# A scan's decayed inputs formed on VectorE from the transposed tile, with decay times step size, in place of a second product on GpSimd

## The chip, the cores and the metric

The kernel runs on one core of one Trainium2 chip. The metric is device time in microseconds (us) per execution. The engines of the core are TensorE (PE in the profile; PEld is its weight load), VectorE (DVE), ScalarE (ACT), GpSimd (POOL) and SyncE (SP, which here only issues transfers). Each works through its own queue in order and waits for the others by semaphores.

## What is computed

One layer of a hybrid block on 512 frames: a retention branch and a Mamba-2 (SSD) branch, merged by gates, then an output projection. The change lies in the SSD branch. Cut to it:

```python
dt = softplus(dt_raw + dt_bias)                 # (b, s, groups, heads per group): the step size
a = dt * (-exp(a_log))
xdt = xs * dt[..., None]
def step(state, inp):                           # over chunks
    xc, bc, cc, ac = inp                        # xc is a chunk of xdt
    acum = cumsum(ac, axis=1)
    ...
    y = einsum('blsg,blsgh,bsghp->blghp', cb, decay, xc)            # inside the chunk
    y = y + einsum('blgn,bghpn->blghp', cc, state) * exp(acum)[..., None]
    tail = exp(acum[:, -1:] - acum)
    state = (state * exp(acum[:, -1])[..., None, None]
             + einsum('bsgn,bsgh,bsghp->bghpn', bc, tail, xc))      # the scan's decayed inputs: tail times xc
    return state, y
```

So a chunk of `xs` is needed twice: times `dt` for the work inside the chunk, and times `dt` and `tail` for the state.

## The kernel before

The kernel does the scan in chunks of 128 frames, so there are TB = 4. Activations lie with channels on the 128 partitions and time along the row. Each projection is a large float32 product done in two parts: weights `wf` arrive by SP (L266), DVE forms combinations of their blocks (L268, L273, L274), ACT rounds them into a high part `whi` (L158), DVE forms the low part `wlo` (L161), and PE runs three products of 128x256 for each block (L256, L257, L258) into the PSUM banks `pb`. There are 7 buffers of `whi` and 6 of `wlo`, so DVE and ACT may run that far ahead of PE. DVE and ACT collect the banks into `o` (L327 to L334).

The program first does the projections and the retention branch (to about 790 us), then the SSD branch (to about 1974 us), then the projections of the branches and the output. In the SSD branch there are 8 groups. Each has four tiles of 128 channels (two heads each), taken in pairs (`jj`, and `e` in the pair): the projections of a pair are formed with a convolution (L754) and a SiLU, and then each tile `y` goes through the scan:

- PE transposes the four chunks of `y` into a PSUM tile `ps` (L796), named `att` in the profile like all tiles of that pool of four.
- DVE multiplies it by `dt` into `xd` (L798).
- POOL multiplies the first three chunks of `xd` by `tail` into `xl` (L801).
- PE forms the new part of each state from `xl` (L805). ACT copies the first state (L808) and DVE chains the others (L812) into `S`.
- SP loads `L` (L818); ACT and DVE turn it into the decay matrix times C and B (L822, L826, L827).
- PE multiplies `xd` by `L` (L831) and `S` by C (L835). DVE adds up (L837 to L840), and POOL adds the squares to a running sum (L845, named `R` in the profile).

`xd`, `xl`, `S`, `L` and `E` have one buffer each. `dt`, `At`, `tail` and `cd` are four parts of one SBUF tile `sst`, filled in the retention stage by `step_sizes` and `decays`, after heads 1 and 2.

What stands where in each engine's queue is set by a scheduler, which plays the whole program through with costs of its own; it weaves the scan's instructions between those of the next projections. A change of one instruction's engine or length can so move others.

Of the kernel before, what the change touches and what calls it, by code (L numbers as in the profile page):

```python
# [8 lines left out]
F32 = mybir.dt.float32  # L9
# [3 lines left out]
ALU = mybir.AluOpType  # L13
# [3 lines left out]
P = 128  # L17
T = 512
TB = T // P
# [118 lines left out]
def hybrid_block(tc, A, out):  # L138
    nc = tc.nc
    PE, ACT, DVE, POOL, SP = nc.tensor, nc.scalar, nc.vector, nc.gpsimd, nc.sync  # L140
# [6 lines left out]
    op = ctx.enter_context(tc.tile_pool(name="op", bufs=2))  # L147
# [6 lines left out]
    def att_tile():  # L154
        return att.tile([P, T], F32, name="att")
# [224 lines left out]
    dt, At, tail, cd = (sst[:, i] for i in range(4))  # L380
# [44 lines left out]
    pe, act, dve, sp = (InOrder(tc, e) for e in (PE, ACT, DVE, SP))  # L425
# [67 lines left out]
    ps = att_tile()  # L493
# [87 lines left out]
    def decays(pool):  # L581

        av = cd.rearrange("p c h -> p (c h)")
        pa = att_tile()
        PE.matmul(pa[:, :TB * SH], tri, av, start=True, stop=True)
        DVE.tensor_copy(At.rearrange("p c h -> p (c h)"), pa[:, :TB * SH])
        pl = att_tile()
        PE.matmul(pl[:, :TB * SH], ones, av, start=True, stop=True)
        DVE.tensor_tensor(tail.rearrange("p c h -> p (c h)"), pl[:, :TB * SH],
                          At.rearrange("p c h -> p (c h)"), op=ALU.subtract)  # L590
        ACT.activation(tail, tail, AF.Exp)
        ACT.activation(cd.rearrange("p c h -> p (c h)"), pl[:, :TB * SH], AF.Exp)
        pf = att_tile()
        for tb in range(TB):
            PE.transpose(pf[:SH, tb * P:(tb + 1) * P], At[:, tb, :], ident)
        both = pool.tile([P, 2, T], F32, name="steps", tag="g")
        Af, Ef = both[:SH, 0, :], both[:SH, 1, :]
        DVE.tensor_copy(Af, pf[:SH, :])
        ACT.dma_start(out=A_d, in_=Af)
        ACT.activation(Ef, pf[:SH, :], AF.Exp)  # L600
        ACT.dma_start(out=E_d, in_=Ef)


    with tc.tile_pool(name="ret", bufs=1) as rp:
        for h in range(NH):
# [73 lines left out]
            for sb in (3, 0, 1, 2):  # L679
                n, sl = T - sb * P, slice(sb * P, (sb + 1) * P)  # L680
                ps = att_tile()
# [25 lines left out]
            for lb in range(TB):  # L707
                ps = att_tile()
# [21 lines left out]
            if h == 2:  # L730
                decays(rp)
# [3 lines left out]
    with tc.tile_pool(name="ssd", bufs=1) as sp:  # L735
# [28 lines left out]
        for g in range(NG):  # L764
# [3 lines left out]
            ps = att_tile()  # L768
# [3 lines left out]
            ps = att_tile()  # L772
# [6 lines left out]
            for jj in range(2):  # L779
# [5 lines left out]
                for e in range(2):  # L785
                    j = j0 + e
                    h0 = 2 * j
                    hs = slice(h0, h0 + 2)
# [5 lines left out]
                    ps = att_tile()  # L794
                    for c in range(TB):
                        PE.transpose(ps[:, c * P:(c + 1) * P], y[:, c * P:(c + 1) * P], ident)  # L796
                    xd = sp.tile([P, TB, 2, 64], F32, name="xd")
                    DVE.tensor_tensor(xd, ps.rearrange("p (c i d) -> p c i d", c=TB, i=2),  # L798
                                      dt[:, :, hs, None].to_broadcast([P, TB, 2, 64]), op=ALU.mult)
                    xl = sp.tile([P, TB - 1, 2, 64], F32, name="xl")  # L800
                    POOL.tensor_tensor(xl, xd[:, :TB - 1], tail[:, :TB - 1, hs, None].to_broadcast([P, TB - 1, 2, 64]),  # L801
                                       op=ALU.mult)
                    ps = att_tile()
                    for c in range(TB - 1):
                        PE.matmul(ps[:, c * P:(c + 1) * P], Bk[:, c, :], xl[:, c].rearrange("p i d -> p (i d)"),  # L805
# [3 lines left out]
                    for c in range(1, TB - 1):  # L809
                        for i in range(2):  # L810
                            d = slice(i * 64, (i + 1) * 64)
# [51 lines left out]
    with tc.tile_pool(name="br", bufs=1) as bp:  # L863
# [27 lines left out]
        for i in range(NP):  # L891
# [3 lines left out]
            if i == ROOT:  # L895
                ps = att_tile()
# [260 lines left out]
```

## Time and profile before

| what | value |
|---|---|
| median of 3 runs | 2657.84 us (2657.81 to 2658.74) |
| the profiled execution | 2656.96 us, its span 2655.1 us |
| busy over the span | PE 2642.9, DVE 2434.9, ACT 1416.2, POOL 221.4 us |
| granted TensorE clock | 0.999 |
| moved by DMA | 371.51 MB, mean 140 GB/s |

The span is the time from the first to the last instruction that the profile shows; the execution's time has some 2 us around it. Busy time is the time in which an engine had at least one instruction under way, so it can hide that an instruction started late. In a row of a group, the two numbers after the first bar are busy us in total and mean ns of one instruction, and behind the second bar stands the idle time of the engine just before them with what ended it. In a row of the timeline the numbers are start and duration in us, and the bracket gives the idle time before it.

### The profile page before, as it was taken

The page shows a single profiled execution, that of the slowest core. Times are in us where ns is not written, and L with a number is a line of the kernel's source. Part 1 is how long each engine was busy: PE and PEld are TensorE (multiplying, and loading weights), DVE is VectorE, ACT ScalarE, POOL GpSimd, SP SyncE. Part 2 cuts the span into 40 slices and gives each one's busy share as a digit, 9 for nine tenths or more (in the row PEclk, how much of TensorE's full clock was granted, in tenths as well). Part 3 has the DMA queues.
Part 4 walks back from the last instruction along what each step waited for, and adds up shares of the span by engine and source line. Part 5 has one row for each costly group of instructions (what it writes and reads, how often), then busy time and mean ns, then how long its engine had stood idle before and what let it go on. Part 6 is the DMA issues. An engine that isn't in the chain of part 4 may idle for free.

```text
span 2655.1 us, 52347 instructions
## 1 busy us (share of the span) xinstructions
PE 2642.9 (100%) x20748; PEld 2548.6 (96%) x20748; DVE 2434.9 (92%) x3892; ACT 1416.2 (53%) x1975; POOL 221.4 (8%) x170
## 2 busy tenths in 40 slices
PE   9999999999999999999999999999999999999998
PEld 5999999999999999999999999999999989999898
DVE  8999989988989999998999999899989999998998
ACT  7444443444446666666666666666674453443544
POOL 0000000000000000010010001000000202100021
PEclk9999999999999999999999999999999999999999
DMA  5333333333333444343444434344464666756534
GB/s 179 99 101 96 108 104 108 104 100 108 104 117 117 135 133 134 119 132 113 133 134 134 134 118 132 112 134 136 134 222 139 229 220 210 251 164 216 176 113 145
DMA packets 182454, 371.51 MB, mean 140 GB/s; under 512 B 21281, under 2 KB 28961, under 8 KB 182209
## 3 DMA queue, kind: packets, MB, share of 16 engines
q1 hardware_dynamic: 167504, 324.77, 38.1%
q0 software_dynamic: 6048, 21.63, 2.3%
q10 hardware_dynamic: 8656, 21.77, 2.1%
q8 instruction: 162, 2.65, 0.4%
q14 instruction: 84, 0.68, 0.1%
HBM read 326.94 MB, written 41.16 MB: 139 GB/s over the span
## 4 chain that ended last, share of the span: by engine, by line
PE 96%; DVE 2%; DMA 1%; ACT 1%; POOL 0%; issue 0%; SPq 0%; DVEq 0%; ACTq 0%
PE pb L258 25%; PE pb L256 24%; PE pb L257 24%; PE att L258 4%; PE att L256 3%; PE att L257 3%; PE pb L254 2%; PE att L831 1%; PE att L712 1%; PE att L835 1%; PE att L254 1%; PE pb L128 1%; PE att L685 1%; PE att L805 1%; PE att L128 1%; DMA r<-in_xT_dram 1%
## 5 line engine op out<-in xcount | busy, mean ns | idle before, releaser
L158 ACT CAST whi<-wf 128x896 fp32r<-128x896 f32 (+1 forms) x960 | 827.9, 907 | 721.1 <-DVE wf L274 365.2
L161 DVE TENSOR_TENSOR wlo<-wf,whi 128x896 fp32r<-128x896 f32 (+1 forms) x960 | 1011.7, 1069 | 76.3 <-PE pb L258 59.9
L258 PE MATMUL pb<-a,wlo 128*128 128x256 f32 (+1 forms) x3296 | 923.2, 291 | 0.5 <-DVE wlo L161 0.5
L257 PE MATMUL pb<-a,whi 128*128 128x256 f32 (+1 forms) x3040 | 874.4, 291 | 0.0
L256 PE MATMUL pb<-a,whi 128*128 128x256 f32 (+1 forms) x3040 | 873.8, 293 | 0.0
L256 PE MATMUL pb<-b,whi 128*128 128x256 f32 x2304 | 654.0, 284 | 0.0
L257 PE MATMUL pb<-b,whi 128*128 128x256 f32 x2304 | 652.6, 284 | 0.0
L258 PE MATMUL pb<-b,wlo 128*128 128x256 f32 x2304 | 649.3, 284 | 0.0
L258 PEld LDWEIGHTS pb<-a,wlo 128*128 128x128 f32 x3296 | 613.7, 191 | 10.4 <-DVE wlo L161 0.7
L256 PEld LDWEIGHTS pb<-a,whi 128*128 128x128 f32 x3040 | 578.9, 191 | 16.5 <-issue 1.5
L257 PEld LDWEIGHTS pb<-a,whi 128*128 128x128 f32 x3040 | 580.0, 191 | 14.0 <-issue 0.8
L257 PEld LDWEIGHTS pb<-b,whi 128*128 128x128 f32 x2304 | 440.3, 191 | 0.0
L256 PEld LDWEIGHTS pb<-b,whi 128*128 128x128 f32 x2304 | 440.2, 191 | 0.0
L258 PEld LDWEIGHTS pb<-b,wlo 128*128 128x128 f32 x2304 | 438.6, 191 | 0.5 <-issue 0.5
L268 DVE TENSOR_TENSOR wf<-wf 128x512 f32<-128x512 f32 x432 | 301.2, 697 | 33.5 <-DMA wf<-in_w_in_dram 25.0
L274 DVE TENSOR_TENSOR wf<-wf 128x256 f32<-128x256 f32 x432 | 187.6, 434 | 0.9
L273 DVE TENSOR_TENSOR wf<-wf 128x256 f32<-128x256 f32 x432 | 188.1, 435 | 0.1
L258 PE MATMUL att<-a,wlo 128*128 128x256 f32 (+1 forms) x480 | 141.4, 304 | 0.0
L801 POOL TENSOR_TENSOR xl<-xd,sst 128x384 f32<-128x384 f32 x32 | 52.6, 1643 | 792.9 <-DVE xd L798 792.9
L257 PE MATMUL att<-a,whi 128*128 128x256 f32 (+1 forms) x384 | 117.9, 310 | 0.0
L256 PE MATMUL att<-a,whi 128*128 128x256 f32 (+1 forms) x384 | 117.8, 310 | 0.0
L254 PE MATMUL pb<-a,whi 128*128 128x512 f32 x256 | 100.6, 398 | 0.0
(273 smaller groups left out, 3163.0 us busy)
## 6 DMA issues: line engine op xcount, KB each, us to landing
wf<-in_w_in_dram SPq DMA_DIRECT2D x703, 256.0 KB, 2.9
wf<-in_w_br_ssd_dram SPq DMA_DIRECT2D x128, 256.0 KB, 3.5
wf<-in_w_out_dram SPq DMA_DIRECT2D x72, 256.0 KB, 2.9
L<-A_d SPq DMA_DIRECT2D x32, 512.0 KB, 4.1
wf<-in_w_br_ret_dram SPq DMA_DIRECT2D x64, 256.0 KB, 3.0
ys_d<-Q ACTq DMA_DIRECT2D x32, 256.0 KB, 2.0
r<-ys_d SPq DMA_DIRECT2D x16, 512.0 KB, 6.8
E<-E_d SPq DMA_DIRECT2D x64, 96.0 KB, 3.1
```

The lines of the kernel that those rows point to most:

```text
L128: ins = getattr(self.engine, name)(*args, **kw).ins
L158: high = ACT.copy(dst_hi, src).ins
L161: return DVE.tensor_tensor(dst_lo, src, dst_hi.bitcast(F32), op=ALU.subtract).ins
L254: PE.matmul(pt[0], wh, both(k, x), start=b not in started, stop=(k == NP - 1), skip_group_check=True)
L256: PE.matmul(o, wh, xh, start=b not in started, stop=False, skip_group_check=True)
L257: PE.matmul(o, wh, xl, start=False, stop=False, skip_group_check=True)
L258: PE.matmul(o, wl, xh, start=False, stop=(k == NP - 1), skip_group_check=True)
L268: first = DVE.tensor_tensor(f2[:, :, 4:6, :], f2[:, :, 1:3, :], f2[:, :, 0:1, :].to_broadcast([P, 2, 2, P]), op=ALU.subtract)
L273: DVE.tensor_tensor(f2[:, :, 0, :], f2[:, :, 2, :], f2[:, :, 4, :], op=ALU.add)
L274: DVE.tensor_tensor(f2[:, :, 6, :], f2[:, :, 3, :], f2[:, :, 0, :], op=ALU.subtract)
L685: PE.matmul(ps[:, :n], ks[a][:, i, sl], qs[b][:, i, sb * P:], start=(i == 0 and m == 0), stop=(i == 1 and m == 2))
L801: POOL.tensor_tensor(xl, xd[:, :TB - 1], tail[:, :TB - 1, hs, None].to_broadcast([P, TB - 1, 2, 64]), op=ALU.mult)
```

## The change

`tail` is multiplied by `dt` once, when both are there. In the scan, DVE now forms `xl` first, from the transposed tile in PSUM times this product, and then `xd` from the same PSUM tile, as before. The product on POOL is gone.

```diff
@@ decays
         ACT.activation(tail, tail, AF.Exp)
+        DVE.tensor_tensor(tail, tail, dt, op=ALU.mult)
         ACT.activation(cd.rearrange("p c h -> p (c h)"), pl[:, :TB * SH], AF.Exp)
@@ the scan of one tile
                     for c in range(TB):
                         PE.transpose(ps[:, c * P:(c + 1) * P], y[:, c * P:(c + 1) * P], ident)
+                    turned = ps.rearrange("p (c i d) -> p c i d", c=TB, i=2)
+                    xl = sp.tile([P, TB - 1, 2, 64], F32, name="xl")
+                    DVE.tensor_tensor(xl, turned[:, :TB - 1],
+                                      tail[:, :TB - 1, hs, None].to_broadcast([P, TB - 1, 2, 64]), op=ALU.mult)
                     xd = sp.tile([P, TB, 2, 64], F32, name="xd")
-                    DVE.tensor_tensor(xd, ps.rearrange("p (c i d) -> p c i d", c=TB, i=2),
-                                      dt[:, :, hs, None].to_broadcast([P, TB, 2, 64]), op=ALU.mult)
-                    xl = sp.tile([P, TB - 1, 2, 64], F32, name="xl")
-                    POOL.tensor_tensor(xl, xd[:, :TB - 1], tail[:, :TB - 1, hs, None].to_broadcast([P, TB - 1, 2, 64]),
-                                       op=ALU.mult)
+                    DVE.tensor_tensor(xd, turned, dt[:, :, hs, None].to_broadcast([P, TB, 2, 64]), op=ALU.mult)
                     ps = att_tile()
```

Lines after the first edit are one higher in the changed kernel: L796 is L797, L805 is L806, L831 is L832, L835 is L836, L837 is L838. The products are L800 (`xl`) and L803 (`xd`), the product of `tail` and `dt` is L592.

The queues move with it. On POOL, from the last product of the retention stage on, before:

```order
L718 TENSOR_TENSOR rs<-rs,mhalf 128x1 x32
L801 TENSOR_TENSOR xl<-xd,sst 128x384 x2
L845 TENSOR_TENSOR R_80<-R_80,K 128x512
L801 TENSOR_TENSOR xl<-xd,sst 128x384 x2
L845 TENSOR_TENSOR R_80<-R_80,K 128x512 x2
```

And in the changed kernel:

```order
L361 MEMSET quarter 128x1
L719 ISA
L719 TENSOR_TENSOR rs<-rs,mhalf 128x1 x32
L846 TENSOR_TENSOR R_80<-R_80,K 128x512 x31
L884 DMA s<-gs_d 128x1024
L872 DMA m_d<-f 128x1024
```

The squared sums now stand there alone. On DVE, in the first pair of the first group, between the first tile's products and the second's, before:

```order
L333 TENSOR_TENSOR o<-o,pb_9083 128x256
L273 TENSOR_TENSOR wf<-wf 128x2x128
L812 SCALAR_TENSOR_TENSOR S<-S,sst,att 128x64 x2
L334 TENSOR_TENSOR o<-pb_9084,o 128x2x256
L274 TENSOR_TENSOR wf<-wf 128x2x128
L812 SCALAR_TENSOR_TENSOR S<-S,sst,att 128x64
L837 SCALAR_TENSOR_TENSOR Q<-Q,dsk,att 128x512
L161 TENSOR_TENSOR wlo<-wf,whi 128x896
L812 SCALAR_TENSOR_TENSOR S<-S,sst,att 128x64
L161 TENSOR_TENSOR wlo<-wf,whi 128x896
L268 TENSOR_TENSOR wf<-wf 128x2x256
L798 TENSOR_TENSOR xd<-att,sst 128x512
```

And in the changed kernel:

```order
L333 TENSOR_TENSOR o<-o,pb_9084 128x256
L813 SCALAR_TENSOR_TENSOR S<-S,sst,att 128x64 x2
L273 TENSOR_TENSOR wf<-wf 128x2x128
L838 SCALAR_TENSOR_TENSOR Q<-Q,dsk,att 128x512
L334 TENSOR_TENSOR o<-pb_9085,o 128x2x256
L813 SCALAR_TENSOR_TENSOR S<-S,sst,att 128x64 x2
L161 TENSOR_TENSOR wlo<-wf,whi 128x896
L274 TENSOR_TENSOR wf<-wf 128x2x128
L800 TENSOR_TENSOR xl<-att,sst 128x384
L803 TENSOR_TENSOR xd<-att,sst 128x512
```

The second tile's products now stand together, with one `wlo` (L161) ahead of them where two stood, and the first tile's sum (L838) sooner. On PE, in the first pair of the second group, around the first tile's products with `xd` (`pb` are the banks of the projections), before:

```order
L258 MATMUL pb_11101<-a_252,wlo 128x256
L256 MATMUL pb_11101<-b_505,whi 128x256
L257 MATMUL pb_11101<-b_505,whi 128x256
L831 MATMUL att<-L,xd 64x128 x8
L835 MATMUL att<-V,S 128x128
L796 MATMUL att<-cc,Q 128x128 x4
```

And in the changed kernel:

```order
L256 MATMUL pb_11100<-a_252,whi 128x256
L257 MATMUL pb_11100<-a_252,whi 128x256
L806 MATMUL att<-xl,S 128x128 x3
L832 MATMUL att<-L,xd 64x128 x8
L836 MATMUL att<-V,S 128x128
L797 MATMUL att<-cc,Q 128x128 x4
```

Before, the products with `xl` (L805) stood 17 rows of projection matmuls ahead of those with `xd`; now they stand directly ahead of them, and the next tile's transposes follow.

## The prediction

> **What bounds the kernel now.** I read the page first, then the busy time in the stage that the change touches, then that stage's waits, then single instructions there. The page's first part and its chain:
>
> ```profile
> span 2655.1 us, 52347 instructions
> PE 2642.9 (100%) x20748; PEld 2548.6 (96%) x20748; DVE 2434.9 (92%) x3892; ACT 1416.2 (53%) x1975; POOL 221.4 (8%) x170
> PE 96%; DVE 2%; DMA 1%; ACT 1%; POOL 0%; issue 0%; SPq 0%; DVEq 0%; ACTq 0%
> ```
>
> TensorE (PE) is never long without a matmul, and it holds 96% of the chain. VectorE (DVE) is next with 92%, so an edit that gives it more work is not free by itself. The edit lies in the SSD stage, about 790 to 1974 us, and in one instruction of the retention stage before it. The busy columns of those stretches, in the order PE, PEld, DVE, ACT, POOL:
>
> ```profile
> 240.00:790.00 550.00, 549.54 (x4388) 540.21 (x4388) 497.26 (x858) 238.38 (x304) 27.54 (x24) 1.00 0.34 106
> 790.00:1974.00 1184.00, 1182.81 (x10053) 1170.42 (x10052) 1090.37 (x1745) 744.00 (x1091) 102.46 (x63) 1.00 0.41 132
> ```
>
> In the SSD stage PE is idle for 1184.00 - 1182.81 = 1.2 us, DVE for 1184.00 - 1090.37 = 93.6 us, and the granted clock is 1.00. So only PE's waits can become shorter here, and there is room on DVE. Does DVE really run ahead, or does its idle time stand in the wrong places? The stage's waits answer that (who waited, for whom, us, times, longest), with the DVE and POOL groups of the stretch 790 to 1990 behind them:
>
> ```profile
> POOL xl L801 <- DVE xd L798: 792.9, 32, 54.1
> DVE wlo L161 <- PE pb L258: 35.2, 21, 3.6
> PEld att L805 <- POOL xl L801: 2.1, 5, 0.6
> PE att L805 <- POOL xl L801: 1.2, 3, 0.4
> ...
> L161 DVE TENSOR_TENSOR wlo<-wf,whi 128x896 fp32r<-128x896 f32 x420 | 460.4, 1113 | 43.1 <-PE pb L258 34.8 <-ACT whi L158 7.9
> L801 POOL TENSOR_TENSOR xl<-xd,sst 128x384 f32<-128x384 f32 x32 | 52.6, 1643 | 792.9 <-DVE xd L798 792.9
> L798 DVE TENSOR_TENSOR xd<-att,sst 128x512 f32<-128x512 f32 x32 | 21.9, 685 | 2.7 <-PE att L796 2.4
> L838 DVE TENSOR_TENSOR E<-att,E 128x384 f32<-128x384 f32 x32 | 17.5, 548 | 0.2 <-PE att L835 0.2
> L839 DVE TENSOR_TENSOR Q<-Q,E 128x384 f32<-128x384 f32 x32 | 17.5, 548 | 0.0
> ```
>
> DVE stops 21 times until PE has read an old low part of the weights (wlo) and so given its buffer back: it has then filled all that it may fill. In this stage PE waits for wlo in no row of that list; what it waits for is POOL's xl, 2.1 us on weight loads and 1.2 us on matmuls. That is the wait which the change takes away.
>
> **The change part by part.** (1) The second product leaves POOL. What its lateness cost PE can be read from the distance of matmul starts, since the busy column hides part of it. The worst of the three places:
>
> ```profile
> 1178.07 0.28 PE L258 MATMUL pb<-b,wlo 128*128 128x256 f32 x1
> 1178.20 0.38 PE L835 MATMUL att<-V,S 128*128 128x128 f32 x2
> 1178.33 0.36 PE L256 MATMUL pb<-a,whi 128*128 128x256 f32 x1
> 1178.54 0.28 PE L257 MATMUL pb<-a,whi 128*128 128x256 f32 x1
> ...
> 1179.72 0.28 PE L258 MATMUL pb<-a,wlo 128*128 128x256 f32 x1
> 1180.44 0.94 PE L805 MATMUL att<-xl,S 128*128 128x128 f32 x6 [0.44 <-POOL xl L801]
> 1181.13 0.36 PE L256 MATMUL pb<-b,whi 128*128 128x256 f32 x1
> 1181.33 0.28 PE L257 MATMUL pb<-b,whi 128*128 128x256 f32 x1
> ```
>
> A start usually follows the last one by 0.12 us; here it is 1180.44 - 1179.72 = 0.72, so 0.60 us are lost. The two others:
>
> ```profile
> 1334.92 0.28 PE L257 MATMUL pb<-b,whi 128*128 128x256 f32 x1
> 1335.48 0.94 PE L805 MATMUL att<-xl,S 128*128 128x128 f32 x6 [0.29 <-POOL xl L801]
> ...
> 1643.97 0.28 PE L258 MATMUL pb<-a,wlo 128*128 128x256 f32 x1
> 1644.68 0.94 PE L805 MATMUL att<-xl,S 128*128 128x128 f32 x6 [0.44 <-POOL xl L801]
> ```
>
> They lose 0.56 - 0.12 = 0.44 and 0.71 - 0.12 = 0.59. Together 1.6 us, which I take as the gain, between 1.2 (PE's idle time) and 3.3 (2.1 + 1.2, as if loads and matmuls waited one after the other).
>
> (2) DVE gets 32 products of 128x384 with one operand in PSUM (att) and one small one (sst). The nearest row is L838, the same shape, also from att: 548 ns. 32 x 0.548 = 17.5 us. The product xd stays at 685 ns, since its operands are the same. The Trainium skill, "Perfetto Trace Analysis", section "Optimizing Scalar/DVE Operations", gives DVE about 60 ns of overhead on SBUF and about 125 ns on PSUM; by that a product from PSUM would be some 65 ns dearer than from SBUF, an estimate of 2 us over 32. The group L839 above, an SBUF product of this width, takes 548 ns like L838, so the measurement goes against it here and I add nothing.
>
> (3) DVE gets something back. While POOL's second product runs, DVE instructions with both operands in SBUF become longer. First and last of 29 such pairs (each over 50 ns beyond its group's median, found by going through all 32 products; the excess adds up to 13.9 us), with the usual lengths below:
>
> ```profile
> 812.37 1.56 POOL L801 TENSOR_TENSOR xl<-xd,sst 128x384 f32<-128x384 f32 x1 [40.14 <-DVE xd L798]
> 813.15 1.32 DVE L268 TENSOR_TENSOR wf<-wf 128x512 f32<-128x512 f32 x1
> ...
> 1943.10 0.83 POOL L801 TENSOR_TENSOR xl<-xd,sst 128x384 f32<-128x384 f32 x1 [35.05 <-DVE xd L798]
> 1943.27 2.62 DVE L161 TENSOR_TENSOR wlo<-wf,whi 128x896 fp32r<-128x896 f32 x2
> ...
> 1176.00 2.08 DVE L161 TENSOR_TENSOR wlo<-wf,whi 128x896 fp32r<-128x896 f32 x2
> 1178.01 0.68 DVE L268 TENSOR_TENSOR wf<-wf 128x512 f32<-128x512 f32 x1
> ```
>
> 1.32 against 0.68, and 2.62 against 2.08 for two. So DVE's net load in the stage rises by 17.5 - 13.9 = 3.6 us (between 3.6 and 17.5). The cover is its 93.6 us of idle time, above all the 35.2 us at a full set of wlo buffers. On the path: nothing. If that cover were gone, up to 17.5 us.
>
> (4) The new product of tail and dt is one 128x256 instruction, once. The nearest row is the subtraction of the same size:
>
> ```profile
> 330.94 0.42 DVE L589 TENSOR_TENSOR sst<-att,sst 128x256 f32<-128x256 f32 x1
> 333.28 0.42 ACT L591 ACTIVATE sst<-sst 128x256 f32<-128x256 f32 x1
> 335.35 0.42 DVE L274 TENSOR_TENSOR wf<-wf 128x256 f32<-128x256 f32 x1
> ```
>
> It stands behind that L274 in the new order. The exponential it waits for ended at 333.70, and DVE comes there at 335.69, so nothing queues behind a wait. 0.42 us on DVE, which idles 550.00 - 497.26 = 52.7 us in that stretch: nothing on the path, at most 0.4. The first product with tail comes 477 us later, at 812.37.
>
> (5) The order of the issue moves. xd now ends 0.55 us later after its transposes, xl ends earlier (before, xd's 0.68 and a POOL product of 1.6 on the mean; now 0.55). The scheduler uses that: PE's products with xl stand nearer to the transposes, and in 13 of 32 head pairs the products with xd stand directly behind them (8 before). POOL's queue then holds only the squared sums here, which need nothing of xl, and SP's loads of L and E keep their number and move by a few places. The number of runs of small matmuls between the large ones goes from 143 to 149; by the rows of (1) a lone product costs 1178.54 - 1178.07 - 2 x 0.12 = 0.23, one in a run of three (1181.33 - 1180.44 - 0.12) / 3 = 0.26, so more runs cost nothing. What does cost is a place at which PE arrives before DVE. The trace cannot show it. Lower bound 0; upper bound one wait of 0.54 us (the mean of the three above) for each of the 32, 17.4 us. DVE's distance ahead of PE speaks for the low end, and 3 waits in 32 is what the present order has, so I take 2 such waits, 1.0 us.
>
> **The sum.** The profiled execution took 2656.96 us, of which 2655.1 is the span; the median of the runs is 2657.84, 0.88 above it. 2656.96 - 1.6 + 0 + 0 + 1.0 = 2656.4, and on the scale of the median 2657.2. Between runs 0.2%, or 5.3 us, is about what can be told from no change; my forecast is inside that.
>
> **The rivals.** *PE waits in the new order* (slower). Place: the products with xl and xd behind the transposes, which now have fewer large matmuls between them. Price: 0.54 us a place. It decides from 13 places on, since 13 x 0.54 = 7.0 eats the 1.6 and adds 5.3. With one in each of 16 pairs of tiles it gives 2657.84 - 1.6 + 8.7 = 2664.9. For it: the two products of a tile now fill DVE for 1.23 us in one go, and both are needed at once at 13 places. Against it: DVE waits for PE and not the other way.
>
> *DVE becomes the bound* (slower). Its idle time could be useless because DVE must catch up right after the products. Then the 17.5 + 0.4 us fall on the path: 2657.84 - 1.6 + 17.9 = 2674.1. With what POOL's absence gives back it is 4.0 instead of 17.9, 2660.2, which is no measurable change; it needs 6.9 of the 17.9 to be exposed. For it: 92% on the page. Against it: 7.9% idle time in the stage itself, and no wait for wlo. The Trainium skill speaks for this rival: the same section says that with DVE saturated it may make sense to move work to Scalar or even GpSimd, and the change goes the other way; the row of the stage shows DVE busy but not saturated.
>
> *PE gains more than its visible waits* (faster). All waits for xl gone is 2657.84 - 3.3 = 2654.5, still no measurable gain. Over 5.3 us would need something that no row shows, such as a luckier order of the small matmuls.
>
> That the product stays on POOL is excluded: the new order has no such row on that engine.
>
> **How the numbers follow.** Forecast, no measurable change: 0.85. PE waits in the new order: 0.08. DVE the bound: 0.04. Faster: 0.03. So faster 0.03, same 0.85, slower 0.12. The low end is 2654.5, all waits for xl gone and none new. The high end is ten new waits instead of two, 2657.84 - 1.6 + 5.4 = 2661.6. Some 2 in 10 lie outside, mostly above.
>
> **What would show it.** POOL's busy time in the stage falls by about 50 us, to the squared sums alone; xl on DVE has 32 instructions of about 548 ns; L268 and L161 no longer show lengths of 1.3 and 1.6 us beside a second product, though some beside the squared sums; DVE's busy time in the stage rises by about 4 us (by more if (3) is wrong); the waits of PE for xl are at most a few tenths and name DVE. It is wrong if the chain in the stage shows DVE for more than a few us, if PE's idle time there goes past 7 us, or if starts of matmuls behind xl or xd lie over 0.5 us apart at more than a dozen places.

## The result and the profile after

| | before | changed |
|---|---|---|
| median, runs of the same chip | 2658.15 us (2657.61 to 2659.86, 6 runs) | 2674.8 us (2673.2 to 2676.24, 6 runs) |
| the profiled execution, its span | 2656.96, 2655.1 us | 2676.24, 2673.9 us |

The ratio is 1.0062, with a 95% interval of 1.0052 to 1.0072: the changed kernel is 16.6 us slower. 2657.2 was forecast, no change, and the range ended at 2661.6.

The head of the page of the changed kernel, span, busy times and the chain by engine:

```profile
span 2673.9 us, 52285 instructions
PE 2648.8 (99%) x20748; PEld 2551.4 (95%) x20748; DVE 2449.1 (92%) x3925; ACT 1417.1 (53%) x1973; POOL 174.8 (7%) x138
PE 34%; DVE 1%; ACT 1%; issue 0%; DVEq 0%; ACTq 0%
```

The chain breaks off early here (its shares add to 36%), so it says nothing of the stage. PE's busy time is 5.9 us more than before in a span 18.8 us longer. The 5.9 us are no more work: the kernel has the same 20748 matmuls. The count of matmuls in a stretch shows better what is lost. The stretches of before, on the changed kernel:

```profile
240.00:790.00 550.00, 549.54 (x4388) 540.20 (x4387) 497.65 (x859) 238.52 (x304) 27.53 (x24) 1.00 0.34 106
790.00:1974.00 1184.00, 1169.75 (x9934) 1156.53 (x9933) 1089.47 (x1745) 732.82 (x1071) 54.98 (x29) 1.00 0.40 127
```

Until 790 us nothing has changed. In the SSD stage PE's idle time rose from 1.2 to 14.2 us. DVE is no busier in this stretch of time than before (1089.47 against 1090.37), though it gets through less of the stage in it; over the whole run it is 14.2 us busier. The stage in windows of 74 us, a steady one and the six that are not (the columns are as above):

```profile
1308.00:1382.00 74.00, 74.00 (x633) 73.28 (x632) 68.87 (x113) 48.03 (x70) 3.31 (x2) 1.00 0.41 128
1382.00:1456.00 74.00, 72.17 (x615) 71.15 (x614) 66.46 (x106) 44.70 (x67) 4.01 (x2) 1.00 0.37 124
1456.00:1530.00 74.00, 71.72 (x610) 70.70 (x609) 67.42 (x109) 45.62 (x66) 3.99 (x2) 1.00 0.41 130
1530.00:1604.00 74.00, 71.96 (x613) 70.95 (x613) 66.34 (x109) 45.31 (x67) 1.31 (x1) 1.00 0.36 107
1604.00:1678.00 74.00, 72.13 (x614) 71.11 (x613) 67.76 (x108) 46.49 (x67) 6.11 (x3) 1.00 0.41 134
1678.00:1752.00 74.00, 72.07 (x611) 71.21 (x610) 64.49 (x103) 44.38 (x66) 0.57 (x1) 0.99 0.33 106
1752.00:1826.00 74.00, 72.34 (x605) 70.79 (x602) 70.84 (x117) 44.37 (x67) 4.94 (x3) 0.98 0.44 140
```

A full window has 633 to 635 matmuls; the next five have 610 to 615. Against 634 they lack 19 + 24 + 21 + 20 + 23 = 107, and at 74.00 / 634 = 0.117 us each that is 12.5 us. They hold the pairs of tiles 8 to 12 of the 16. The last row lacks 29 more, 3.4 us, of which some 1.2 us is a lower clock (0.98; the last section shows the place). The rest is lost at single places before 1234 us.

What waits there, in the stage (first the waits by engine and line, then groups of instructions, with idle time and releaser behind the second bar):

```profile
ACT L L823 <- DMA L<-A_d: 39.1, 14, 6.2
DVE L L828 <- ACT L L827: 34.1, 17, 5.7
DVE wlo L161 <- PE pb L258: 5.8, 8, 1.3
...
L256 PE MATMUL pb<-a,whi 128*128 128x256 f32 (+1 forms) x1712 | 478.6, 287 | 9.1 <-ACT whi L158 4.7 <-DVE o L333 2.6 <-ACT o L330 1.5
L832 PE MATMUL att<-L,xd 128*64 128x128 f32 x512 | 35.6, 282 | 3.9 <-issue 3.9
L800 DVE TENSOR_TENSOR xl<-att,sst 128x384 f32<-128x384 f32 x32 | 17.6, 550 | 2.3 <-PE att L797 2.1
```

The same waits and the products with L before:

```profile
ACT L L822 <- DMA L<-A_d: 23.4, 11, 3.9
DVE L L827 <- ACT L L826: 6.8, 8, 1.2
...
L831 PE MATMUL att<-L,xd 128*64 128x128 f32 x512 | 35.0, 279 | 0.0
```

PE hardly waits for `xl` any more (one place, 0.3 us). It waits for `whi`, for the adding up of the projection (L330, L333), and 3.9 us at the products with L (`att<-L,xd`: the products of `xd` with `L`). Those are marked "issue", so the profile names no releaser; the engines below show it. DVE waits 34.1 us for ACT's exponential (6.8 before), and its 35.2 us of waiting for PE's old `wlo`, which the prediction took for its lead, have shrunk to 5.8.

One of the five pairs in the trace, first PE and SP, then ACT, then DVE:

```profile
1483.99 1.09 PE L832 MATMUL att<-L,xd 128*64 128x128 f32 x16
1498.31 1.09 PE L832 MATMUL att<-L,xd 128*64 128x128 f32 x16 [1.22 <-issue]
1510.26 0.38 PE L256 MATMUL pb<-a,whi 128*128 128x256 f32 x1 [0.43 <-ACT whi L158]
1511.63 0.36 PE L256 MATMUL pb<-a,whi 128*128 128x256 f32 x1 [0.62 <-DVE o L333]
...
1485.12 0.33 SPq L819 DMA_DIRECT2D L<-A_d  x1
...
1489.66 2.45 ACT L823 ACTIVATE L<-L,sst 128x128 f32<-128x128 f32 x8 [5.31 <-DVE xd L803]
1492.13 1.28 ACT L785 ACT_TABLE_LOAD   x1
1493.43 1.15 ACT L785 ACTIVATE K<-o 128x512 f32<-128x512 f32 x2
1494.60 1.28 ACT L827 ACT_TABLE_LOAD   x1
1495.89 1.06 ACT L827 ACTIVATE L<-L 128x1024 f32<-128x1024 f32 x1
...
1496.98 1.23 DVE L828 TENSOR_TENSOR L<-L,S 128x1024 f32<-128x1024 f32 x1 [5.00 <-ACT L L827]
```

`L` has one buffer. The first tile's products with it run from 1483.99 to 1485.08. SP issues the reload at 1485.12, and ACT, whose next instruction in order is the ReLU on the new `L`, stands idle for 5.31 us until 1489.66 (the name behind the arrow is that of a DVE product which happened to end at 1489.59; the ReLU does not read it, and the wait is for the transfer, 4.4 us at the median). Then come eight ReLUs (2.45), the SiLU of `z` with its table (2.4), the exponential with its table (2.3), and DVE's product (1.23), for which DVE has stood still for 5.00 us. It ends at 1496.98 + 1.23 = 1498.21, and at 1498.31 PE begins the second tile's products; their other operand, `xd`, had been ready since 1489.59. From the first tile's first product to the second's there are 14.3 us, in which PE's queue holds 12.9 to 13.0 us of work. So PE stands, and so does DVE, with all the weight splits that are queued behind L828; ACT's own rounding of weights (L158) stands behind the exponential in its queue. PE's waits for `whi` and L333 (0.43 and 0.62 us) follow 12 us later. That they come of this stop is read from the order of the queues; it was not tried at this place.

The same place before:

```profile
1483.20 1.28 ACT L784 ACT_TABLE_LOAD   x1 [5.22 <-DVE o L334]
1488.23 2.46 ACT L822 ACTIVATE L<-L,sst 128x128 f32<-128x128 f32 x8
...
1494.86 1.22 DVE L827 TENSOR_TENSOR L<-L,S 128x1024 f32<-128x1024 f32 x1
...
1483.46 1.09 PE L831 MATMUL att<-L,xd 128*64 128x128 f32 x16
1498.06 1.09 PE L831 MATMUL att<-L,xd 128*64 128x128 f32 x16
```

The SiLU of `z` (L784) is done while the reload is under way, not between the ReLUs and the exponential; `L` is ready at 1494.86 + 1.22 = 1496.08, and PE needs it at 1498.06, 2.0 us later.

Call what PE has to do from the first tile's products with L to the second's, less the length of the way through `L` (products 1.1, reload 4.4 and its issue, ACT's work up to the exponential, DVE's 1.23), the **room** of a pair. It is an estimate, worked out from the order of the instructions and the durations of the rows. Before, it is 0.4 to 3.0 us in all 16 pairs. In the changed kernel it is -1.3 to -1.4 us in exactly the five pairs 8 to 12 (6.7 us in all), and 0.7 to 2.7 elsewhere. The trace agrees: in those five the second tile's products begin 0.1 us after `L` is ready, in the eleven others 1.1 to 3.2 us after, and before the change 1.3 to 4.1 us after in all 16. Both sides of the sum count. In the five pairs the trace has 84 or 85 projection matmuls between the products, and ACT's part of the way is 7.3 us; elsewhere it has 87 to 110 matmuls and 3.5 to 6.7 us (the two pairs with 87 are those with 3.5 and 4.2 us).

### The profile page after: what moved, and what is told of

It is laid out like the page before. It is cut to its first block, busy times and chain, and to the rows that moved or that the text cites. A ratio compares the mean times of both kernels' runs of the same rounds, so it can differ in the third digit from the quotient of the medians.

```text
span 2673.9 us, 52285 instructions
## 1 busy us (share of the span) xinstructions
PE 2648.8 (99%) x20748; PEld 2551.4 (95%) x20748; DVE 2449.1 (92%) x3925; ACT 1417.1 (53%) x1973; POOL 174.8 (7%) x138
## 5 line engine op out<-in xcount | busy, mean ns | idle before, releaser
L158 ACT CAST whi<-wf 128x896 fp32r<-128x896 f32 (+1 forms) x960 | 827.8, 907 | 688.2 <-DVE wf L274 356.0
L161 DVE TENSOR_TENSOR wlo<-wf,whi 128x896 fp32r<-128x896 f32 (+1 forms) x960 | 1004.4, 1059 | 60.8 <-PE pb L258 29.3
L268 DVE TENSOR_TENSOR wf<-wf 128x512 f32<-128x512 f32 x432 | 299.4, 693 | 31.4 <-DMA wf<-in_w_in_dram 20.5
L274 DVE TENSOR_TENSOR wf<-wf 128x256 f32<-128x256 f32 x432 | 196.8, 456 | 1.1
L273 DVE TENSOR_TENSOR wf<-wf 128x256 f32<-128x256 f32 x432 | 185.1, 428 | 0.3
L846 POOL TENSOR_TENSOR R<-R,K 128x512 f32<-128x512 f32 x31 | 57.9, 1868 | 1160.5 <-ACT K L845 1151.6
L823 ACT ACTIVATE L<-L,sst 128x128 f32<-128x128 f32 x256 | 78.4, 389 | 49.4 <-DMA L<-A_d 39.1
```

Of the source, the lines that this page charges most:

```text
L158: high = ACT.copy(dst_hi, src).ins
L161: return DVE.tensor_tensor(dst_lo, src, dst_hi.bitcast(F32), op=ALU.subtract).ins
L268: first = DVE.tensor_tensor(f2[:, :, 4:6, :], f2[:, :, 1:3, :], f2[:, :, 0:1, :].to_broadcast([P, 2, 2, P]), op=ALU.subtract)
L273: DVE.tensor_tensor(f2[:, :, 0, :], f2[:, :, 2, :], f2[:, :, 4, :], op=ALU.add)
L274: DVE.tensor_tensor(f2[:, :, 6, :], f2[:, :, 3, :], f2[:, :, 0, :], op=ALU.subtract)
L823: bent = ACT.activation(L[:, i, c, :], L[:, i, c, :], AF.Relu, scale=-1.0, bias=At[:, c, h0 + i:h0 + i + 1]).ins
```

## The experiments

Theory O: the time is lost because the scheduler, given the changed instructions, wrote another order, which in five pairs leaves too little room for `L`. Theory D: it is lost because DVE has 17.6 us more to do. Experiments 1 to 4 shared one set of runs of the kernel before (2657.18 us), 5 to 8 another (2657.28), 9 and 10 a third (2658.44), 11 and 12 a fourth (2657.32).

**1. More room in the five pairs.** The changed kernel, with the second tile's first product with L held behind a later projection matmul, 100 behind the first tile's (the scheduler sees the edge and orders the rest anew; the code is shortened here, as it is in the excerpts below):

```diff
+    FAR = {...}            # per late tile of pairs 8 to 12: the projection matmul ahead of its products
+    def main(ins):         # called with each projection matmul
+        if ins.ins.name in FAR:
+            behind(first_L[FAR[ins.ins.name]], ins.ins.name)
```

> The changed kernel with one thing more: in the five pairs of tiles where PE stalled at the products with L (pairs 8 to 12), the second tile's products with L are put behind a projection matmul that stands 100 after the first tile's (they stood 84 to 87 after it). Room in the order is then positive in all 16 pairs (0.4 us and more). Theory O, that the order left less PE work between the two tiles' products than the way through L needs (reload 4.45, ACT 7.3, products 2.5 us): each of the five pairs gives back about 2.3 us, 2674.8 - 12 = 2663 us (2660 to 2667). Theory D, that VectorE's added 17.5 us is the bound: the work is unchanged, 2672 to 2676 us.

2668.84 us, ratio 1.0043 (1.0031 to 1.0056). The stalls at the products with L are gone (0.0 us in the group), but only about 5 of the 16.6 us came back: PE now waits 5.7 us for `wlo` and 3.2 for `whi` and the adding up. The room of the five pairs is 0.4 to 2.6 us; DVE still waits 18.6 us for the exponential. Neither forecast holds; the room in PE's order is not all that counts.

**2. The two products in the other order.** `xd` first, then `xl`; the same work for every engine:

```diff
+                    xd = sp.tile([P, TB, 2, 64], F32, name="xd")
+                    DVE.tensor_tensor(xd, turned, dt[:, :, hs, None].to_broadcast(...), op=ALU.mult)
                     xl = sp.tile([P, TB - 1, 2, 64], F32, name="xl")
                     DVE.tensor_tensor(xl, turned[:, :TB - 1], ...)
-                    xd = sp.tile([P, TB, 2, 64], F32, name="xd")
-                    DVE.tensor_tensor(xd, turned, dt[:, :, hs, None].to_broadcast(...), op=ALU.mult)
```

> The changed kernel with its two VectorE products in the other order, xd ahead of xl. The instructions and their work are the same, the scheduler's order is another: room is negative in one pair only (-1.4 us, against five pairs in the changed kernel). Theory O: four pairs less at 2.3 us, 2674.8 - 9 = 2665 us (2660 to 2668). Theory D: 2672 to 2676 us. A third theory, X, that xd comes late now because xl stands ahead of it: the stalls at the products with xd go, those at the products with xl grow.

2662.02 us, ratio 1.0018 (1.0009 to 1.0027). Swapping two neighbours gives the scheduler another start, and its order has one pair with negative room (-1.4, pair 12) instead of five. PE's one wait at the products with L is in that pair:

```profile
L832 PE MATMUL att<-L,xd 128*64 128x128 f32 x512 | 35.0, 279 | 1.2 <-issue 1.2
```

DVE has the whole load that theory D blames, and the time is 4.8 us above the kernel before in the same set of runs, where the changed kernel lies 16.6 above it. As O expects. Theory X, also on record, fails: no wait for `xl` takes the place of those that went.

**3. Less room in the kernel before.** 30 projection matmuls of each pair from 1 to 14 (counted from 0) that stood ahead of the second tile's products with L are put behind them:

```diff
+    NEAR = {...}           # 30 projection matmuls per pair -> the tile behind whose products with L they go
+    def main(ins):
+        if ins.ins.name in NEAR:
+            behind(ins.ins, last_L[NEAR[ins.ins.name]])
```

> The kernel before, its work unchanged and GpSimd's product kept, but with 30 projection matmuls of each pair from the second to the fifteenth put behind the second tile's products with L, so that these stand nearer to the first tile's (59 to 90 matmuls instead of 91 to 114). Room is negative in six pairs, -6.0 us in sum (-6.8 in the changed kernel). Theory O: slower than before by 6 to 14 us, 2664 to 2672 us, with PE's waits at the products with L. Theory D: no work is added to VectorE, 2657 to 2660 us.

2664.81 us, ratio 1.0029 (1.0019 to 1.0039): slower, at the low end for O. It is weak evidence: six pairs have a room of -0.6 to -1.9, but the scheduler answered with another order on ACT too, and PE lost only 0.8 us at the products with L and 2.6 behind ACT's copy of a bank (L341).

**4. DVE's load alone.** The kernel before, with a spare DVE product of the shape of `xl`, from the same PSUM tile; GpSimd's product stays:

```diff
+                    spare_xl = sp.tile([P, TB - 1, 2, 64], mybir.dt.bfloat16, name="xs")
+                    DVE.tensor_tensor(spare_xl, ps.rearrange("p (c i d) -> p c i d", c=TB, i=2)[:, :TB - 1],
+                                      tail[:, :TB - 1, hs, None].to_broadcast([P, TB - 1, 2, 64]), op=ALU.mult)
```

> The kernel before with a spare VectorE product of 128x384 from the transposed tile for each of the 32 tiles, into a bfloat16 tile that nothing reads; GpSimd's product stays. VectorE gets 17.5 us more and nothing back. Room in the order is positive in all pairs (1.0 us and more). Theory O: 2656 to 2661 us. Theory D: 2670 us and more.

2658.93 us, ratio 1.0006 (0.9997 to 1.0014). DVE's rows show the load:

```profile
790.00:1974.00 1184.00, 1183.01 (x10058) 1171.12 (x10057) 1107.65 (x1774) 744.40 (x1091) 84.85 (x63) 1.00 0.40 132
...
L801 DVE TENSOR_TENSOR xs<-att,sst 128x384 bf16<-128x384 f32 x32 | 17.5, 545 | 0.0
```

DVE is busy for 1107.65 us of the stage, 17.3 more than before, and PE is idle for 1.0 us of it (1.2 before). Theory D falls: the added load costs nothing that can be measured in an order with room in every pair.

**5. The changed kernel in the order of before.** Every engine's instructions are held to the order of the kernel before, with `xl` directly ahead of `xd` on DVE:

```diff
+    made = {i.name: i for i in nc.cur_bb.bb.instructions}
+    for names in ORDERS:                    # one list per engine
+        for first, then in zip(names, names[1:]):
+            behind(made[then], first)
```

> The changed kernel's instructions (xl on VectorE from the transposed tile, decay times step size), with every engine held to the order of the kernel before; xl stands directly ahead of xd on VectorE. Theory O (the new order of issue costs the time: too little TensorE work between the two tiles' products with L, while L is reloaded and made again): the order with room everywhere is back, so the 16.6 us go, 2655 to 2658 us, as before or up to 1.6 us faster, since the three waits for GpSimd's xl go too. Theory D (the added VectorE products cost the time): VectorE has the same added work, so 2672 to 2676 us.

2656.29 us, ratio 0.9995 (0.9986 to 1.0004). All 16.6 us are back.

```profile
PE 2642.6 (100%) x20748; PEld 2548.7 (96%) x20748; DVE 2437.6 (92%) x3925; ACT 1416.8 (53%) x1975; POOL 168.5 (6%) x138
...
1456.00:1530.00 74.00, 73.83 (x631) 73.06 (x630) 69.11 (x112) 46.87 (x68) 2.71 (x2) 1.00 0.42 133
```

**6. The work of before in the order of the changed kernel** (POOL keeps its own order; held in the same way):

> The kernel before's work (xl on GpSimd from xd, no tail times dt) in the order that the changed kernel has on TensorE, VectorE, ScalarE and the DMA queues. Theory O: the five pairs of tiles with 12.9 to 13.0 us of TensorE work between the products with L stall as in the changed kernel, 2672 us or more (up to 2682, since xl now comes from GpSimd at places set for VectorE). Theory D: VectorE has its old load, so 2657 to 2660 us.

2680.67 us, ratio 1.0087 (1.0073 to 1.0101). The order alone costs the time: 23.4 us above the kernel before, 6.8 more than the changed kernel. PE now also waits 4.7 us for GpSimd's `xl`:

```profile
L831 PE MATMUL att<-L,xd 128*64 128x128 f32 x512 | 35.0, 279 | 5.1 <-issue 5.1
L805 PE MATMUL att<-xl,S 128*128 128x128 f32 x192 | 27.8, 280 | 4.7 <-POOL xl L801 4.7
```

**7. The changed kernel in its own order, with next to no product for `xl`** (the rest of `xl` is left out and stays zero):

```diff
-                    DVE.tensor_tensor(xl, turned[:, :TB - 1], ...)
+                    DVE.tensor_tensor(xl[:, :1, :, :16], turned[:, :1, :, :16],
+                                      tail[:, :1, hs, None].to_broadcast([P, 1, 2, 16]), op=ALU.mult)
```

> The changed kernel in its own order, but with VectorE's product for xl cut to 16 columns of one chunk per head (most of xl is left out and stays zero): about 14 us less on VectorE, all waits and places as they are. Theory O: the way from L's load over ScalarE to the products with L is as long as in the changed kernel, so 2668 to 2675 us. Theory D: the added load is nearly gone, so 2657 to 2660 us.

2674.05 us, ratio 1.0064 (1.0051 to 1.0076): as the changed kernel. The product was cut from 550 to 185 ns, 11.7 us in all (not 14), and nothing came of it.

```profile
L801 DVE TENSOR_TENSOR xl<-att,sst 128x32 f32<-128x32 f32 x32 | 5.9, 185 | 2.4 <-PE att L799 2.1
...
L833 PE MATMUL att<-L,xd 128*64 128x128 f32 x512 | 35.0, 279 | 4.6 <-issue 4.6
```

**8. The engine alone.** In the kernel before, `xl` is formed by DVE from `xd` in SBUF:

```diff
-                    POOL.tensor_tensor(xl, xd[:, :TB - 1], ...)
+                    DVE.tensor_tensor(xl, xd[:, :TB - 1], ...)
```

> The kernel before with the engine alone changed: xl is still xd times the decay, read from SBUF, but on VectorE in place of GpSimd. The order that comes of it leaves 0.2 us or more of TensorE work over the way through L in every pair of tiles (0.2 and 0.3 in two of them, 0.7 or more elsewhere), unlike the changed kernel's minus 1.3 in five. Theory O: 2657 to 2664 us. Theory D: the same added VectorE work as in the changed kernel, so 2672 to 2676 us.

2663.66 us, ratio 1.0025 (1.0015 to 1.0034): within O's range, at its upper end. No product with L is waited for; PE waits 3.4 us for `wlo`, 1.3 for L331 and 1.2 for `S`. Again an order of its own, with small waits elsewhere. What its 6.4 us come of is not shown. PE waits for `wlo`, which is DVE's work, so the added load may have a part in it here.

Experiments 5 and 6 show that the order is the cause. Which part of it, the next ones ask.

**9. A smaller reload.** The changed kernel in its own order, held; from the second tile on only one block of `L` is loaded (64 KB, an eighth of the 512 KB; the text on record says a sixteenth, which is wrong):

```diff
+                    part = slice(0, 2) if whole else slice(0, 1)
+                    cols = T if whole else P
-                    SP.dma_start(out=L.rearrange(...), in_=A_d[hs, :].partition_broadcast(P))
+                    SP.dma_start(out=L[:, part].rearrange(...)[:, :, :cols],
+                                 in_=A_d[hs, :][part, :cols].partition_broadcast(P))
```

> The changed kernel in its own order on every engine, but from the second tile on the reload of L brings one block of 128 columns for one head in place of 1024 columns for two (a sixteenth of the bytes; the rest of L keeps what stood there, so the output is not the reference's). Every instruction, its place and its waits stay; only the way from the first tile's products with L to the second's gets some 2 us shorter (the load took 4.4 us). If that way through the single L is what costs the time: the five pairs that lacked 1.3 to 1.4 us have 0.6 us or more to spare, so 2657 to 2664 us. If the order costs the time in another way (where the chunks of the split, the transposes or the products with xl and xd stand): 2670 to 2676 us, as the changed kernel.

2665.54 us, ratio 1.0028 (1.0017 to 1.0039): between the two. The size of the cut was misjudged. The transfer, the same pair's ReLUs, and DVE's product:

```profile
L<-A_d SPq DMA_DIRECT2D x31, 64.0 KB, 3.5
...
1480.19 1.09 PE L836 MATMUL att<-L,xd 128*64 128x128 f32 x16
...
1484.57 2.46 ACT L827 ACTIVATE L<-L,sst 128x128 f32<-128x128 f32 x8 [4.00 <-DMA L<-A_d]
...
1491.89 1.23 DVE L832 TENSOR_TENSOR L<-L,S 128x1024 f32<-128x1024 f32 x1 [3.45 <-ACT L L831]
```

An eighth of the bytes still took 3.5 us against 4.4, and from the first product to the first ReLU there are now 4.4 us against 5.7. So the way got 1.3 us shorter, not 2, and the room of the five pairs is about 0. PE no longer stalls at the products with L, but DVE still waits 3.45 us there, and in the five windows PE is still idle for 0.6 to 0.9 us each (1.8 to 2.3 in the changed kernel), behind `whi` and L333. With no room there is no wait at the products themselves, but what is queued behind DVE's product (L832 here) is still late.

**10. A longer way in the kernel before**, held to its own order:

```diff
+                    for _ in range(3):
+                        ACT.activation(L, L, AF.Relu)
                     ACT.activation(L, L, AF.Exp, scale=-1.0)
```

> The kernel before, each engine held to its own order, with three spare ReLUs over the whole of L (128x1024, about 1.06 us each) put ahead of ScalarE's exponential in every tile; they change no value. ScalarE is idle 47% of the span, and its work as such is hidden. If the way through L is what counts: it gets 3.2 us longer, so the 16 pairs of tiles, which have 0.4 to 3.0 us to spare, then lack 0.2 to 2.8 us each, 18 us in all, and the time rises by that or, as in the changed kernel where 6.7 us of lack cost 16.6 us, by 2.5 times that: 2675 to 2705 us. If not: 2657 to 2660 us.

2726.2 us, ratio 1.0256 (1.0242 to 1.027): 67.8 us, more than the range given, 3.7 times the lack of 18 us. PE's waits are spread over everything that DVE and ACT deliver:

```profile
790.00:1995.00 1205.00, 1162.18 (x9765) 1142.65 (x9764) 1069.68 (x1687) 807.62 (x1140) 107.38 (x59) 1.00 0.38 122
...
DVE L L829 <- ACT L L828: 79.7, 30, 3.9
...
L805 PE MATMUL att<-xl,S 128*128 128x128 f32 x180 | 26.1, 281 | 10.4 <-POOL xl L801 10.4
```

ACT is idle for a third of this stretch, so it is not its load. DVE waits 79.7 us for the exponential, and everything behind that wait is late. So is what stands behind the spare ReLUs in ACT's own queue: PE waits 5.4 us for `whi` and 5.0 us for ACT's copy of `S`. The two were not tried apart.

**11. No reload.** The changed kernel in its own order, held; `L` is loaded for the first tile alone, and the loads of the other 31 are left out:

```diff
+                    if whole:                      # the first tile only
                         SP.dma_start(out=L.rearrange(...), in_=A_d[hs, :].partition_broadcast(P))
+                    whole = False
```

> The changed kernel in its own order, but L is loaded in the first tile alone (the reloads of the other 31 tiles are left out, so the output is not the reference's). The cut load before it still took 3.5 us against 4.4, so that the way through L was only some 1.3 us shorter, the five pairs had just about nothing to spare, and VectorE still waited 3.45 us there in place of 5.00. Without the reload ScalarE can bend L again as soon as the first tile's products have read it, and the way gets 3.5 to 4.4 us shorter than in the changed kernel. If that way, with VectorE's queue that stands behind it, is the whole cost: 2655 to 2660 us. If half of the cost comes from another place in the order: 2663 to 2667 us, as with the cut load.

2658.74 us, ratio 1.0003 (0.9994 to 1.0012). With ACT free to begin as soon as the old `L` is read, the whole loss is gone, in the same order and with the same DVE load. The windows that lacked 19 and 24 matmuls are full:

```profile
1382.00:1456.00 74.00, 74.00 (x634) 73.40 (x634) 69.55 (x111) 45.94 (x68) 3.99 (x2) 1.00 0.36 115
1456.00:1530.00 74.00, 74.00 (x634) 73.41 (x633) 70.54 (x114) 46.08 (x67) 4.00 (x2) 1.00 0.39 120
...
L831 DVE TENSOR_TENSOR L<-L,S 128x1024 f32<-128x1024 f32 x32 | 39.2, 1224 | 15.7 <-ACT L L830 15.7
```

**12. One spare ReLU** instead of three:

> As with three spare ReLUs over L in every tile of the kernel before, but one (about 1.06 us). If only the lack counts: the pairs have 0.4 to 3.0 us to spare, so that one pair lacks 0.7 us and the 15 others keep 0.4 us or more, 2657 to 2663 us. If every added us on the way through L counts: a third of the 67.8 us that three of them cost, 2680 us.

2667.35 us, ratio 1.0037 (1.0024 to 1.0049): 10.0 us, where room alone as the threshold gave at most 5.7 and a constant price per microsecond 22.6. The cost grows faster than the added time (10 for 1.06 us, 68 for 3.2), and it begins before the room of a pair is used up: 15 of the 16 still had 0.4 us or more. PE does not wait at the products with L at all here; it waits 3.3 us for GpSimd's `xl` and 2.7 us for `wlo`, which come late.

## Why the prediction was wrong

Step (5), the order of the issue, failed; the other terms were right or off the path. It was priced at two new waits of 0.54 us, 1.0 us in all; the order cost 23 us with GpSimd's `xl` (experiment 6) and 16.6 with DVE's. It was wrong in two ways. The first is the releaser. The step looked for places at which PE comes to the products with `xl` and `xd` before DVE has formed these two, and such waits hardly occur (0.3 us for `xl`). PE does stand at the products with `xd`, but for their other operand, `L`. The order moved projection matmuls out of the stretch between two products with L, and the SiLU of `z` into the way through `L`. The prediction put that way at nothing: of it, it says only that SP's loads of `L` keep their number and move by a few places. The second is the price of a place, 0.54 us, the mean of three waits for `xl`. A way that goes through four engines and one buffer can lack more, and its price is not the wait at its end: in the five pairs, a lack of 6.7 us by the estimate goes with some 12.5 us lost, 2.5 us a pair. The queues of DVE and ACT stand behind the wait, and what they owe PE comes late: in pair 12 PE's wait of 1.72 us is for a `whi` that stands behind the exponential in ACT's queue. How the loss divides between the two queues was not tried.

The argument for the low end was that DVE waits for PE. It says nothing of this way, on which DVE waits for ACT and ACT for the reload. In the kernel before, ACT already waited 23.4 us for the reload in 11 places and DVE 6.8 us for the exponential in 8; with these rows the way could have been found and added up. The prediction did not read them.

- (1) Right in kind: the three waits for GpSimd are gone. What it is worth alone cannot be told: experiment 5, which has the gain without the order, is 1.0 us faster, inside its interval (-3.7 to +1.1 us).
- (2) Right: 32 products of 550 ns, 17.6 us (17.5 forecast).
- (3) Right in the order of before: DVE's busy time on the page rises by 2437.6 - 2434.9 = 2.7 us there (3.6 forecast). In the changed kernel it rises by 14.2. The new order puts POOL's squared sum beside L274 in 15 places, none before, and L274 then takes some 1.3 us and not 0.42 (at 1507.90 us it takes 1.33, beside a squared sum that began at 1507.65). So what L161 and L268 give back is partly lost again. L274 on the changed kernel and in experiment 5 (434 ns before):

```profile
L274 DVE TENSOR_TENSOR wf<-wf 128x256 f32<-128x256 f32 x432 | 196.8, 456 | 1.1
...
L274 DVE TENSOR_TENSOR wf<-wf 128x256 f32<-128x256 f32 x432 | 183.9, 426 | 0.9
```

  That such a load is hidden where the order has room is as forecast: experiment 5 hides its 2.7 us, experiment 4 hides 17.3.
- (4) Hidden, as forecast: up to 790 us PE's row is that of before.
- The rivals. *PE waits in the new order* had 0.08. Its kind was right (the order), its releaser and price were not: it gave 2664.9. *DVE becomes the bound* gave 2674.1, next to the result, for a reason that is not there: experiments 4, 5 and 7 exclude it, so that this number was luck. The Trainium skill, "Perfetto Trace Analysis", section "Optimization Strategy", says that the same gap repeating on the engine that should be saturated can mean too few buffers for the next tile. The trace agrees: in four of the five pairs PE has a gap of 0.9 to 1.2 us at the same product, in the fifth one of 1.7 us just ahead of it, all behind a tile with one buffer.
- Of the signs named, PE's idle time of more than 7 us came true.

The cause is settled as far as the order (5, 6) and the way through `L` in it (9, 11) go. Experiment 11 also takes away 31 transfers of 512 KB, and experiment 9 most of their bytes; that these matter by themselves was not tried apart, but experiment 5 has them all, in the other order, and loses nothing. Nor was a second buffer of `L` tried in this order. Why the scheduler brought the products together is not shown.

## What to carry to other kernels

When a scheduler writes the order, an edit that frees one engine can cost more through the new order than through its own instructions: compare the two kernels with the order held before blaming the edit. For each tile with one buffer, add up the whole way from its last reader through reload and remaking to its next reader, over all engines, and set it against the bound engine's work in between; check both orders for the smallest difference. A wait in an in-order queue is paid by all that stands behind it, so such a way should have some room to spare, not just none to lack: here, one more microsecond on ways that nearly all still had room cost 10 us (experiment 12).

## What the runs showed of the hardware

A transfer of an eighth of the bytes was only 20% shorter: 64 KB landed 3.5 us after the issue, 512 KB 4.4 us. So some 0.9 us for 448 KB, and, if time grows evenly with size, about 3.4 us that do not depend on it, an estimate from these two. The Trainium skill, "DMA: Bandwidth & Descriptors", section "Anatomy of one DMA — SWDGE (gpsimd) path", gives about 2.0 us fixed and bytes over 436 GB/s, for transfers that GpSimd issues; by that, as an estimate, 1.0 us would lie between the two, which agrees, while the fixed part measured here, for a load that SP issues beside other traffic, is larger.

A stop of PE cost more than its length at one place of the changed kernel. PE waited 1.72 us there, and in the 4 us after it the granted clock was 0.63 (0.94 in the 4 us after those):

```profile
1750.24 0.39 PE L256 MATMUL pb<-a,whi 128*128 128x256 f32 x1 [1.72 <-ACT whi L158]
...
1750.00:1754.00 4.00, 3.76 (x26) 3.28 (x27) 4.00 (x6) 2.86 (x5) 0.00 (x0) 0.63 0.02 4
```

4 x (1 - 0.63) = 1.5 us more. In finer windows the clock is 0.50 from 1751.07 to 1754.49 us, 3.41 us long, and 1.00 on either side. After the wait of 1.49 us at 1802 it stayed at 1.00. Experiment 10 shows what may tell the two apart. In it the clock also falls to 0.50 for stretches of 3.41 us, which begin at 1029.90, 1354.17, 1838.86 and 2002.70 us (the last is two of them long). These starts lie 95, 142 and 48 times 3.413 us apart, as if the clock were set once in each such stretch of a fixed grid. In the stretch ahead of each drop PE was idle for 1.9 to 2.5 of the 3.41 us, and for 1.72 in the one ahead of 1751.07. On the same grid the wait at 1802 falls into two stretches, with at most 1.1 us idle in one. Where the limit lies is not settled: behind 1.67 us idle there was a drop in experiment 1, behind 1.63 us in experiment 10 and 1.72 us in experiment 6 there was none (the grid of experiment 6 is taken from the drop at its end). The Trainium skill, "TensorE: Matmul & The Clock Gate", section "HAM oscillation — how this bites in real kernels", puts the limit at gaps of over 3.4 us. The trace differs here: a wait of half that length was followed by the drop.
